# Hybrid decoder step on one core: the key scores of the dilated attention with the loop over the four column quarters innermost

## The chip, the cores and the metric

The kernel runs on one core of a Trainium2 chip. The metric is the device time of one launch in microseconds; the median of three runs before the change is 1605.24 us (1603.45 to 1611.88).

## What is computed

One inference step of a two-layer decoder trunk for a prompt (256 tokens) and a sample group (8 batches of 4 tokens), with the same weights: a gated-linear-attention layer, then a layer of dilated sliding-window attention over a shared key/value cache; each layer has a half-step SwiGLU feed-forward part before and after its mixer. The part that matters here is the attention of the samples. For each of the three window groups (distances 1, 4 and 16 between keys, 128 steps back) every sample token is scored against the cached keys:

```python
def dilated_group_sample(q, k_ctx, v_ctx, dil, steps, wb):
    T = q.shape[1]
    idx = wb + np.arange(T)[:, None] - dil * np.arange(steps + 1)[None, :]
...
    kg = k_ctx[:, idx]
    vg = v_ctx[:, idx]
    s = jnp.einsum('bthe,btjhe->bhtj', q, kg, preferred_element_type=jnp.float32) * DIL_SCALE
    p, lse = masked_softmax(s, jnp.asarray(valid)[None, None])
    o = jnp.einsum('bhtj,btjhe->bthe', p, vg.astype(jnp.float32))
    return o, lse.transpose(0, 2, 1)
```

Keys and values are read from cache_k and cache_v (8 batches, 2048 rows of 16 heads by 64), in float32.

## The kernel before

All weights and cache rows come through one stream of tiles, "raw", with 11 buffers (RAW_BUFS, class Stream). SyncE issues the transfers in the order of one job list; a transfer into a buffer waits until the work that last read it is done (for keys, TensorE's transposes at L1430; for values, TensorE's products at L1521). A job of cached rows is 1 MB or 0.75 MB and comes in two transfers of 512 KB (128 rows of 4 KB) or 384 KB (96 rows).

The samples' attention is a loop of 21 steps, x = 0 to 20 (L1542). Two batches are handled per iteration of four steps, so there are four iterations; the four steps of an iteration are (g, tp) = (1, 0), (1, 1), (2, 0), (2, 1), where g is the window group whose rows are loaded (the tiles of g = 1 serve the nearest group and part of the widest as well) and tp a pair of tokens. In a step:

- `keys` (L1420), called for each of the two batches (bp), takes the raw rows, transposes them on TensorE into PSUM (tile pa), ScalarE and VectorE copy them to kt, and GpSimd adds the new key's column (L1439).
- `key_scores` (L1442) multiplies the keys of the step before with the queries (tile qz, kept in the memory of xh and xl) into one PSUM bank, pb, and VectorE masks the result into Sc. It stands between the two calls of `keys`. There are eight calls with g = 1 and eight with g = 2.
- `pieces` (L1395) lets through one piece of the prompt's own attention (scores, softmax, spread, values), three times a step from x = 5 on.
- from x = 5 on, one of the four steps of `outputs` (L1511) multiplies weights with the values that the stream delivers five steps behind the keys.

The order of TensorE's products in this part is fixed: the helper `mm` (L1311, recorded at L1312) and `transpose` (L1314, recorded at L1315) pin each instruction behind the one written before it. So in the profile all products of this part stand at L1312 and all transposes at L1315, and the tiles tell them apart: pb<-kt are the key scores.

A product of the key scores has 32 columns of weights (queries of one batch and one half of the heads), and tile_position=(0, 32 * ...) puts it in one of the four 32-column quarters of the array; its output lies on the 32 partitions of that quarter. For each c4 (four pieces of 128 features) and each quarter there is one product when g = 2 (194 columns of keys), and there are three when g = 1: 258 columns, then 66, then 64 read with a step of four. Each float32 product is two passes on TensorE, each with a weight load of its own: a call with g = 1 is 48 products and 96 passes, a call with g = 2 is 16 products and 32 passes. A call is named a burst below.

```python
            for c4 in range(4):
                for hp in range(2):
                    for bp in range(2):
                        c, q = 4 * hp + c4, 32 * (2 * bp + hp)
```

Of the kernel before, what the change touches and what calls it, by code (L numbers as in the profile page):

```python
# [115 lines left out]
class Stream:  # L116
    """Raw tiles arrive in the order of the job list, by pieces; weights are split into two float32r parts."""
# [37 lines left out]
    def rows(self, i):  # L155
        """The raw pieces of a job and its k-th rows."""
        v = [self.raw.pop(x) for x in self.of[i]]
        return v, [t[:, k, :] for t in v for k in range(t.shape[1])]

    def part(self, low="dve"):  # L160
        """The next part of a weight split, if it is on its way."""
        x = self.parts[self.np]
        if x >= self.nd:
            return None
        self.np += 1
        i = self.pieces[x][0]
        self.split_part(self.split.setdefault(i, Weight()), self.jobs[i], self.raw.pop(x), f"{x}", low)
        self.freed.add(x)
        self.release()
        return True  # L170
# [10 lines left out]
    def aside(self, t, j):  # L181
        """A weight through a tile outside the stream."""
        v = t.rearrange("p (k c) -> p k c", c=j["nc"])
        self.load(v, j, 0, j["nk"])
        return v

    def prep(self, i):
        """All weights up to job i, as far as they are on their way."""
        self.pump()
        while self.np < len(self.parts) and self.pieces[self.parts[self.np]][0] <= i and self.part():  # L190
            pass

    def more(self, n, low="dve"):
        """The next n parts."""
        self.pump()
        while n and self.np < len(self.parts) and self.part(low):
            n -= 1

    def fill(self, limit=None):
        """The adaLN tiles that stand next in the list."""  # L200
        while self.nx < len(self.jobs) and self.jobs[self.nx]["kind"] == "ada":
            if limit is not None:
                if limit == 0:
                    return
                limit -= 1
            i = self.nx
            self.prep(i + 1)
            self.nx += 1
            self.handlers["ada"](self.jobs[i], self.rows(i)[1])
            self.free(i)  # L210
# [17 lines left out]
def weave(main, extra, lead=0, span=None):  # L228
    """extra spread evenly among main, after its first lead jobs."""
    if span is not None:  # L230
        return weave(main[:span], extra, lead) + main[span:]
    out = list(main[:lead])
    rest = main[lead:]
    n, m = len(rest), len(extra)
    k = 0
    for i, j in enumerate(rest):
        while k < m and k * n <= i * m:
            out.append(extra[k])
            k += 1
        out.append(j)  # L240
    out.extend(extra[k:])
    return out
# [64 lines left out]
def cache_job(I, name, g, b, tp, key):  # L307
    c = I[name][b].rearrange("s h e -> s (h e)")
    if g == 1:
        v = c[1536:2048, :].rearrange("(j t) f -> j t f", t=4)  # L310
    else:
        # the last 32 of the 128 rows stand in the first group's tiles too
        v = c.rearrange("(j t) f -> j t f", t=16)[0:J2]
    return dict(kind="r", key=key, src=v[:, 2 * tp:2 * tp + 2, :], nk=2, nc=D, rows=v.shape[0])


def body(tc, I, O, C, dbg=None):
# [17 lines left out]
    def bankB():  # L335
        return psB.tile([P, 512], F32, name=nm("pb"), tag="pb", bufs=3)
# [13 lines left out]
    # ---------------------------------------------------------------- constants and small inputs  # L350
# [23 lines left out]
    def pin(chain, ins):  # L374
        """Instructions of a chain keep their order on their engine."""
        last = chains.get(chain)
        if last is not None:
            tc.add_manual_dep(ins.ins, last.ins.name, mybir.DependencyInfo(mybir.DependencyClass.NoSync,
                              mybir.DependencyReason.DATA), reason="order")
        chains[chain] = ins  # L380
        return ins
# [54 lines left out]
    # ---------------------------------------------------------------- adaLN  # L436
# [37 lines left out]
    def ada_side(l, mod, tiles):  # L474
        """The first parts of an adaLN product, through tiles outside the stream."""
# [11 lines left out]
    def affine(gain, bias, l, msh, msc):  # L487
        """Scale and shift of modulate() after a LayerNorm's gain and bias."""
# [15 lines left out]
    def overlapped(m, last):  # L504
        """The steps of one chunk with the last step of the one before."""
        next(m)
        if last:
            next(last, None)
        next(m)
        return m  # L510

    def modulated(c, src, aff, hi, lo):
        """hi + lo = src * scale + shift, chunk c, in three steps."""
        s, b = aff
# [12 lines left out]
    # ---------------------------------------------------------------- products with a weight tile  # L527
# [13 lines left out]
    def project_chunkwise(group, xhi, xlo):  # L541
        """Several column tiles at once, chunk by chunk of x, as the chunks appear."""
# [4 lines left out]
    # ---------------------------------------------------------------- post-norm  # L547
    class Post:
        def __init__(self, g, late, eng):
            """The first chunks, late in number, come before the pivot."""  # L550
# [18 lines left out]
        def chunk(self, c, ps):  # L569
            zc = self.sublayer(c, ps)  # L570
            if c < 2:
                # a quarter of the features gives a pivot within two deviations of the mean
# [58 lines left out]
        def center(self, n):  # L631
            """The next weight's low part stands after n chunks."""
# [17 lines left out]
    class Final(Post):  # L650
        """The last LayerNorm, with the tokens on the partitions."""
# [37 lines left out]
        def finish(self):  # L689
            """Gain and bias: y * rstd + (bias - mean * rstd * gain), y with its gain already."""  # L690
# [23 lines left out]
    def post_norm(post, l, s, nxt):  # L714
        """nxt: list of (hi, lo); what is returned makes those after the first."""
# [23 lines left out]
    # ---------------------------------------------------------------- SwiGLU  # L739
    SIDE = {(0, 1): (0, 5), (0, 2): (1, 2), (1, 1): (1, 5)}  # L740

    def first_group(xh, xl):
        """The first products, as the shifts and scales of two chunks at a time arrive."""
# [127 lines left out]
    # ---------------------------------------------------------------- gated linear attention  # L871
    def gla(xh, xl):
# [9 lines left out]
        def flat(name, tag=None, bufs=1):  # L882
            """The prompt's rows of the four heads, then the samples' rows of the four heads."""
# [84 lines left out]
        def gram(x_k, x_q, idx, sidx):  # L968
            """The scores of one level, for the pairs that its mask names."""
# [52 lines left out]
        def decayed_keys():  # L1022
            """k times the decay from its row to the end of the rows."""
# [17 lines left out]
        def decayed_keys_t():  # L1041
# [8 lines left out]
            # the samples' rows four times over: high, high, low, low  # L1050
# [20 lines left out]
        def v_transposed(m, vt):  # L1071
# [12 lines left out]
            # the samples' rows four times over: high, low, high, low  # L1084
# [39 lines left out]
        # rows of the prompt  # L1124
# [32 lines left out]
        # rows of the samples, all heads and batches as one tile of rows  # L1157
# [37 lines left out]
        # normalization over a head's values, gate  # L1195
# [22 lines left out]
    # ---------------------------------------------------------------- shared keys and values  # L1218
    def rotate(ps, tab, outs):
        """Rotary encoding of two heads: the swapped halves by copies, their signs in the table."""  # L1220
# [62 lines left out]
    # ---------------------------------------------------------------- dilated attention  # L1283
    def dilated(KT, Vt, Vs, xh, xl):
# [25 lines left out]
        # the products of this part keep the order in which they stand here  # L1310
# [6 lines left out]
        # ---- the prompt, two heads at a time, in the two halves of the array  # L1317
        def scores(c):
            """In three steps."""
# [28 lines left out]
        def spread(c, i, e):  # L1348
            """The transposed weights of a head."""
# [52 lines left out]
        # ---- the samples, two batches at a time; rows are (batch, half of the heads, head, token)  # L1402
# [17 lines left out]
        def keys(pr, g, tp, bp):  # L1420
            """The transposed keys of two tokens, the new key behind them."""
# [20 lines left out]
        def key_scores(g, tp, kc, qz, Sc):  # L1442
            n = P + 1 if g == 1 else N2
            ps = bankB()
            for c4 in range(4):
                for hp in range(2):
                    for bp in range(2):
                        c, q = 4 * hp + c4, 32 * (2 * bp + hp)
                        k_ = kc[bp][hp][:, c4]
                        mm(ps[q:q + 32, 0:2 * n], lhsT=qz[:, g, c, bp, :], rhs=k_.rearrange("p u j -> p (u j)"),  # L1450
                           start=(c4 == 0), stop=(c4 == 3 and g == 2), tile_position=(0, q))
                        if g == 1:
                            mm(ps[q:q + 32, 258:324], lhsT=qz[:, 0, c, bp, :], rhs=k_[:, :, 96:129], start=False, stop=False,
                               tile_position=(0, q))
                            mm(ps[q:q + 32, 324:388], lhsT=qz[:, 2, c, bp, :], rhs=k_[:, :, 0:P:4], start=False,
# [17 lines left out]
        def softmax(pr, Sc):  # L1473
            """The weights: of the new rows, and for each token on the first group's tiles."""
# [5 lines left out]
            # on the first group's tiles: its own weights, the second group's last rows and the nearest rows  # L1480
# [5 lines left out]
            # the new rows: on the rows of all batches, zero where they belong to others  # L1486
# [24 lines left out]
        def outputs(pr, PT, W1, W2):  # L1511
            """In four steps, and the gathering of the heads."""
# [74 lines left out]
    # ---------------------------------------------------------------- the two layers  # L1587
# [76 lines left out]
```

## Time and profile before

| | |
|---|---|
| median of 3 runs | 1605.24 us |
| profiled execution: its own time, and its span | 1603.45 us, 1603.5 us |
| TensorE matmul busy | 1524.3 us, 95% |
| VectorE, ScalarE, GpSimd busy | 58%, 44%, 16% |
| granted clock, mean | 0.979 |
| transfers: bytes, mean rate | 342.72 MB, 214 GB/s |
| the cached rows (samples' attention), loop of 21 steps | about 1107 to 1323 us of the span |

The page gives busy time and share of each engine, the chain of work that ended last, and the costliest groups of instructions. PE is TensorE's matmul side and PEld its weight loads; because passes are pipelined and their ends modelled, a PE busy share near 1 does not say that the array streams all the time. A row of the window view has the stretch and its length, the busy time of PE, PEld, VectorE (DVE), ScalarE (ACT) and GpSimd (POOL) with their instructions, the granted clock, the busy share of the 16 DMA engines and the rate in GB/s at which they moved data. A row of the groups has line, engine, operation, tiles, shape and count, then busy time in us, the mean ns of one, and the idle time before it. The timeline merges consecutive instructions of one line and tile; "x96" is the number of passes.

### The profile page before, as it was taken

How to read it: one execution, taken by the hardware profiler on the slowest of the kernel's cores; microseconds unless marked ns; L12 is line 12 of the kernel's file. 1: busy time of each engine (PE TensorE's matmuls, PEld its weight loads, DVE VectorE, ACT ScalarE, POOL GpSimd, SP SyncE). 2: the span in 40 equal slices, each digit the busy share in tenths (PEclk: the TensorE clock that was granted, in tenths of full speed). 3: DMA queues.
4: the chain of work that ended last, by engine and by line, in shares of the span. 5: the costliest groups of instructions: out<-in, count | busy, mean ns of one | idle time of the engine just before them, and what ended most of it. 6: DMA issues, size and time to landing. Idle time of an engine off the chain costs nothing.

```text
span 1603.5 us, 31330 instructions
## 1 busy us (share of the span) xinstructions
PE 1524.3 (95%) x12564; PEld 1363.0 (85%) x12564; DVE 928.1 (58%) x1887; ACT 706.2 (44%) x1138; POOL 263.3 (16%) x408
## 2 busy tenths in 40 slices
PE   6999999999889999999999999899999988899996
PEld 4999997888869999988999999698766647899995
DVE  4544446596785444468544445765554577845556
ACT  2444333745635443336444434585333244444432
POOL 0000034002450000343000022424231112300001
PEclk8999999999989999999999999999999999999998
DMA  9966776545856677774556575775698996555430
GB/s 311 321 223 223 253 233 202 176 158 172 289 196 199 220 242 265 245 226 153 188 183 210 179 246 176 230 251 165 210 299 251 286 326 245 176 173 166 150 101 30
DMA packets 238820, 342.72 MB, mean 214 GB/s; under 512 B 12743, under 2 KB 202385, under 8 KB 238674
## 3 DMA queue, kind: packets, MB, share of 16 engines
q1 hardware_dynamic: 236210, 333.41, 64.4%
q0 software_dynamic: 2048, 7.14, 1.1%
q8 instruction: 98, 1.61, 0.4%
q14 instruction: 48, 0.39, 0.1%
q10 hardware_dynamic: 416, 0.17, 0.0%
HBM read 332.42 MB, written 8.26 MB: 212 GB/s over the span
## 4 chain that ended last, share of the span: by engine, by line
PE 82%; DVE 9%; DMA 4%; ACT 3%; issue 2%; POOL 1%; SPq 0%; DVEq 0%; ACTq 0%; POOLq 0%
PE pa L530 21%; PE pa L531 21%; PE pa L532 21%; PE pb L1312 5%; PE pd L449 3%; PE pa L1315 3%; PE pa L1312 2%; DMA raw<-in_cache_k_dram 1%; DMA raw<-in_w_ada_dram 1%; PE pa L973 1%; DVE z L639 1%; DVE lo L178 1%; DMA w<-in_w_ffn_up_dram 1%; DVE xm L516 1%; DVE xl L525 1%
## 5 line engine op out<-in xcount | busy, mean ns | idle before, releaser
L530 PE MATMUL pa<-xh,hi 128*128 128x288 f32 x1888 | 560.4, 301 | 12.9 <-ACT xh L523 9.5
L531 PE MATMUL pa<-xl,hi 128*128 128x288 f32 x1888 | 562.5, 298 | 3.1 <-DVE xl L525 2.6
L532 PE MATMUL pa<-xh,lo 128*128 128x288 f32 x1888 | 559.6, 297 | 3.9 <-DVE lo L178 3.9
L178 DVE TENSOR_TENSOR lo<-raw,hi 128x1024 fp32r<-128x1024 f32 (+1 forms) x345 | 414.4, 1209 | 226.8 <-ACT hi L176 220.0
L176 ACT ACTIVATE hi<-raw 128x1024 fp32r<-128x1024 f32 x350 | 358.6, 1035 | 254.5 <-PE pa L531 233.6
L530 PEld LDWEIGHTS pa<-xh,hi 128*128 128x128 f32 x1888 | 356.5, 190 | 26.6 <-ACT xh L523 10.4
L531 PEld LDWEIGHTS pa<-xl,hi 128*128 128x128 f32 x1888 | 359.1, 190 | 6.5 <-DVE xl L525 4.6
L532 PEld LDWEIGHTS pa<-xh,lo 128*128 128x128 f32 x1888 | 358.9, 190 | 5.4 <-DVE lo L178 4.9
L530 PE MATMUL pa<-hh,hi 128*128 128x288 f32 x704 | 209.6, 298 | 0.0
L532 PE MATMUL pa<-hh,lo 128*128 128x288 f32 x704 | 208.3, 296 | 0.0
L531 PE MATMUL pa<-hl,hi 128*128 128x288 f32 x704 | 208.0, 296 | 0.0
L810 DVE TENSOR_TENSOR sa<-pa,sa 128x288 f32<-128x288 f32 x88 | 39.7, 454 | 180.3 <-PE pa L532 174.5
L530 PEld LDWEIGHTS pa<-hh,hi 128*128 128x128 f32 x704 | 132.6, 188 | 4.3 <-issue 2.1
L532 PEld LDWEIGHTS pa<-hh,lo 128*128 128x128 f32 x704 | 132.4, 188 | 0.2
L531 PEld LDWEIGHTS pa<-hl,hi 128*128 128x128 f32 x704 | 132.4, 188 | 0.1
L811 ACT ACTIVATE hh<-sa 128x288 fp32r<-128x288 f32 x88 | 38.8, 445 | 133.9 <-DVE sa L810 131.0
L584 POOL TENSOR_TENSOR z<-z,lnpiv 128x288 f32<-128x288 f32 x6 | 4.7, 803 | 487.9 <-ACT lnpiv L579 487.9
L809 ACT ACTIVATE sa<-pa 128x288 f32<-128x288 f32 x88 | 35.0, 402 | 92.9 <-PE pa L532 92.8
L449 PE MATMUL pd<-raw,cT 128*32 128x256 f32 x1008 | 70.4, 384 | 4.4 <-ACT adas L455 4.4
L1435 ACT ACTIVATE kt<-pa 128x512 f32<-128x512 f32 (+1 forms) x64 | 34.4, 543 | 83.4 <-PE pa L1315 70.1
L1315 PEld LDWEIGHTS pa<-ident,raw 128*128 128x128 f32 (+1 forms) x512 | 50.1, 141 | 20.5 <-issue 8.0
L1315 PE MATMUL pa<-ident,raw 128*128 128x128 f32 (+1 forms) x512 | 59.8, 265 | 4.2 <-DVE kt L1433 1.6
(354 smaller groups left out, 1839.3 us busy)
## 6 DMA issues: line engine op xcount, KB each, us to landing
raw<-in_w_ffn_up_dram SPq DMA_DIRECT2D x172, 512.0 KB, 5.0
raw<-in_w_ada_dram SPq DMA_DIRECT2D x110, 512.0 KB, 4.9
raw<-in_w_ffn_down_dram SPq DMA_DIRECT2D x80, 512.0 KB, 4.8
raw<-in_cache_k_dram SPq DMA_DIRECT2D x32, 512.0 KB, 7.5
raw<-in_cache_v_dram SPq DMA_DIRECT2D x32, 512.0 KB, 7.5
raw<-in_w_in_a_dram SPq DMA_DIRECT2D x24, 512.0 KB, 5.3
raw<-in_w_q_b_dram SPq DMA_DIRECT2D x24, 512.0 KB, 4.5
raw<-in_cache_k_dram SPq DMA_DIRECT2D x32, 384.0 KB, 8.4
```

The costliest lines, as they stand in the source:

```text
L176: self.pin("act", self.nc.scalar.activation(hv, src, AF.Copy))
L178: self.pin(low, eng.tensor_tensor(out=lo, in0=src, in1=hv.bitcast(F32), op=ALU.subtract))
L449: T.matmul(ps[32 * q:32 * q + 32, :], lhsT=cT[:, k, :], rhs=raw[kk][:, 256 * q:256 * q + 256], start=(k == 0), stop=(k == DC - 1), tile_po ...
L530: ins = [T.matmul(ps, lhsT=whi, rhs=xhi, start=first, stop=False), T.matmul(ps, lhsT=whi, rhs=xlo, start=False, stop=False), T.matmul(ps, ...
L531: T.matmul(ps, lhsT=whi, rhs=xlo, start=False, stop=False),
L532: T.matmul(ps, lhsT=wlo, rhs=xhi, start=False, stop=last)]
L809: A.activation(sa, pa[:, 0:NT], AF.Silu)
L810: V.tensor_tensor(out=sa, in0=pu[:, 0:NT], in1=sa, op=ALU.mult)
L811: A.activation(hh[:, m, :], sa, AF.Copy)
L1312: pin("pe", T.matmul(*a, **k))
L1315: pin("pe", T.transpose(*a))
L1435: A.activation(dst, pt, AF.Copy)
```

## The change

The loop over the four quarters becomes the innermost one. Before, the three products of a quarter follow each other and then comes the next quarter; after, the first product of all four quarters, then the second of all four, then the third. The products, their operands, their start and stop flags and the bank stay as they are. With g = 2 there is one product per quarter and the order is the old one. The diff also strips comments and docstrings elsewhere in the file, which moves no instruction.

```diff
         def key_scores(g, tp, kc, qz, Sc):
             n = P + 1 if g == 1 else N2
             ps = bankB()
+            quarters = [(hp, bp) for hp in range(2) for bp in range(2)]
+
             for c4 in range(4):
-                for hp in range(2):
-                    for bp in range(2):
+                for kind in range(3 if g == 1 else 1):
+                    for hp, bp in quarters:
                         c, q = 4 * hp + c4, 32 * (2 * bp + hp)
                         k_ = kc[bp][hp][:, c4]
-                        mm(ps[q:q + 32, 0:2 * n], lhsT=qz[:, g, c, bp, :], rhs=k_.rearrange("p u j -> p (u j)"),
-                           start=(c4 == 0), stop=(c4 == 3 and g == 2), tile_position=(0, q))
-                        if g == 1:
+                        if kind == 0:
+                            mm(ps[q:q + 32, 0:2 * n], lhsT=qz[:, g, c, bp, :], rhs=k_.rearrange("p u j -> p (u j)"),
+                               start=(c4 == 0), stop=(c4 == 3 and g == 2), tile_position=(0, q))
+                        elif kind == 1:
                             mm(ps[q:q + 32, 258:324], lhsT=qz[:, 0, c, bp, :], rhs=k_[:, :, 96:129], start=False, stop=False,
                                tile_position=(0, q))
+                        else:
                             mm(ps[q:q + 32, 324:388], lhsT=qz[:, 2, c, bp, :], rhs=k_[:, :, 0:P:4], start=False,
                                stop=(c4 == 3), tile_position=(0, q))
```

TensorE, first burst with g = 1 (step x = 1), its first c4; kt_12144 and kt_12145 hold the two halves of the heads of batch 0, kt_12176 and kt_12177 those of batch 1, so the four names are the four quarters; 32x258, 32x66 and 32x64 are the three products:

```order
 L1312 MATMUL pb_12240<-kt_12144,xh_12117 32x258
+L1312 MATMUL pb_12240<-kt_12176,xh_12117 32x258
+L1312 MATMUL pb_12240<-kt_12145,xh_12117 32x258
+L1312 MATMUL pb_12240<-kt_12177,xh_12117 32x258
 L1312 MATMUL pb_12240<-kt_12144,xh_12117 32x66
+L1312 MATMUL pb_12240<-kt_12176,xh_12117 32x66
+L1312 MATMUL pb_12240<-kt_12145,xh_12117 32x66
+L1312 MATMUL pb_12240<-kt_12177,xh_12117 32x66
 L1312 MATMUL pb_12240<-kt_12144,xh_12117 32x64
-L1312 MATMUL pb_12240<-kt_12176,xh_12117 32x258
-L1312 MATMUL pb_12240<-kt_12176,xh_12117 32x66
 L1312 MATMUL pb_12240<-kt_12176,xh_12117 32x64
```

The products of the other three quarters with 258 columns move up ahead of the first quarter's shorter ones; four quarters now stand side by side in each kind.

TensorE, the end of the same burst in the changed kernel and the transposes behind it (raw_11893 and raw_12039 are key rows of the step's second batch):

```order
L1312 MATMUL pb_12240<-kt_12145,xh_12117 32x66
L1312 MATMUL pb_12240<-kt_12177,xh_12117 32x66
L1312 MATMUL pb_12240<-kt_12144,xh_12117 32x64
L1312 MATMUL pb_12240<-kt_12176,xh_12117 32x64
L1312 MATMUL pb_12240<-kt_12145,xh_12117 32x64
L1312 MATMUL pb_12240<-kt_12177,xh_12117 32x64
L1315 MATMUL pa_12314<-ident,raw_11893 128x128
L1315 MATMUL pa_12314<-ident,raw_12039 128x128
```

What stands behind the burst is unchanged. The rows of SyncE, ScalarE, VectorE and GpSimd are in the old order too; the only wait that moves is that of the products with kt_12176 and kt_12177 for GpSimd's new-key columns, which now stand second and fourth in the burst, not fourth and tenth.

## Rows read from the trace of the kernel before

**Rows 1.** The page's head and its first part, busy time by engine.
```profile
span 1603.5 us, 31330 instructions
PE 1524.3 (95%) x12564; PEld 1363.0 (85%) x12564; DVE 928.1 (58%) x1887; ACT 706.2 (44%) x1138; POOL 263.3 (16%) x408
```

**Rows 2.** Windows over the samples' attention: busy time by engine, clock, DMA share, GB/s.
```profile
1110.00:1180.00 70.00, 68.55 (x778) 50.95 (x780) 35.07 (x113) 21.69 (x45) 21.04 (x86) 1.00 0.71 213
1180.00:1230.00 50.00, 48.73 (x510) 31.67 (x506) 25.53 (x102) 14.59 (x32) 10.34 (x36) 1.00 0.91 281
1230.00:1310.00 80.00, 76.16 (x798) 46.77 (x792) 49.69 (x191) 30.34 (x72) 12.98 (x35) 1.00 1.01 301
1310.00:1330.00 20.00, 15.72 (x94) 7.35 (x95) 14.45 (x46) 11.40 (x24) 2.48 (x4) 0.85 1.06 366
```

**Rows 3.** Timeline of TensorE, 1115 to 1135 and 1126 to 1148 us: bursts and transposes.
```profile
1115.15 7.94 PE L1312 MATMUL pb<-kt,xh 128*32 128x258 f32 x96
1123.03 3.48 PE L1315 MATMUL pa<-ident,raw 128*128 128x128 f32 x32
1126.43 7.94 PE L1312 MATMUL pb<-kt,xh 128*32 128x258 f32 x96
1134.31 3.14 PE L1315 MATMUL pa<-ident,raw 96*128 96x96 f32 x32
1137.38 1.52 PE L1312 MATMUL pb<-kt,xh 128*32 128x194 f32 x32
```

**Rows 4.** Groups by shape, 1110 to 1330 us: passes and weight loads of the key scores.
```profile
L1312 PE MATMUL pb<-kt,xh 128*32 128x258 f32 x128 | 30.4, 393 | 0.0
L1312 PE MATMUL pb<-kt,xl 128*32 128x64 f32 x128 | 25.1, 286 | 0.0
L1312 PE MATMUL pb<-kt,xl 128*32 128x66 f32 x128 | 17.8, 220 | 0.0
L1312 PE MATMUL pb<-kt,xl 128*32 128x194 f32 x128 | 6.6, 330 | 1.1 <-ACT kt L1435 1.1
L1312 PEld LDWEIGHTS pb<-kt,xl 128*32 128x32 f32 x512 | 26.1, 109 | 13.2 <-issue 1.8 <-POOL pe L1342 1.8
```

**Rows 5.** What SyncE's transfers wait for, 1110 to 1310 us: us, times, longest.
```profile
SPq L144 <- PE pa L1315: 113.2, 40, 11.4
SPq L144 <- PE pa L1312: 21.4, 14, 5.9
```

**Rows 6.** What TensorE waits for, 1110 to 1310 us: us, times, longest.
```profile
PE pa L1315 <- DVE kt L1433: 1.6, 3, 0.8
PE pb L1312 <- ACT kt L1435: 1.1, 1, 1.1
...
PE pa L1315 <- DMA raw<-in_cache_k_dram: 0.3, 1, 0.3
```

**Rows 7.** The chain that ended last, in order of time, around 1230 us.
```profile
1230.71 7.72 DMA raw<-in_cache_k_dram
1238.49 12.20 DMA raw<-in_cache_k_dram
```

**Rows 8.** Instructions of GpSimd's line 1439, 1110 to 1310 us: who waited for it.
```profile
  POOL kt L1439: 10.2, 1
  ACT kt L1435: 2.6, 2
  PEld pb L1312: 0.2, 1
```

**Rows 9.** Windows in which TensorE is often idle: same columns as Rows 2.
```profile
1320.00:1330.00 10.00, 7.49 (x34) 4.78 (x35) 7.90 (x17) 6.96 (x14) 0.00 (x0) 0.70 1.06 403
1350.00:1360.00 10.00, 5.89 (x42) 4.98 (x44) 9.93 (x18) 4.87 (x7) 3.51 (x3) 1.00 0.43 130
1360.00:1370.00 10.00, 6.38 (x74) 3.33 (x66) 7.77 (x12) 3.69 (x8) 7.11 (x7) 0.92 0.71 225
```

## The prediction, made before the changed kernel was run

> **What bounds the kernel now.** I read the page's busy times first [rows 1]: TensorE is busy for 95% of the span, far ahead of every other engine, so work taken from it can count. That is an average; what a saving is worth must be read where it falls. The change touches only the key scores, so the second view is the window view of the samples' attention [rows 2], where the reader is to see two different limits in one stage. From 1110 to 1180 us TensorE is busy for 68.55 of 70 us while the DMA engines are busy for 0.71 of the time at 213 GB/s: TensorE sets the pace. From 1230 to 1310 us the DMA share is 1.01 at 301 GB/s: the transfers of the cached rows are at their limit, and TensorE, with 76.16 of 80 us, is only just as long. Between them, 1180 to 1230, the share is 0.91. The third view is who waits for whom. SyncE's transfers wait 113.2 us for TensorE's transposes to give a raw buffer back and 21.4 us for the value products [rows 5], while TensorE waits next to nothing, 0.3 us of it for cached keys [rows 6]. So TensorE drives the transfers; but the chain that ended last already runs through two transfers of cached keys, 7.72 and 12.20 us, at 1230 us [rows 7]. Both limits are close to each other there.
>
> **The bursts now.** A burst with g = 1 takes 7.94 us for 96 passes and one with g = 2 takes 1.52 us for 32 [rows 3]. Per pass that is 83 ns against 47 ns. The longer products of g = 1 (258 columns, not 194) cannot be the reason, since two thirds of its passes have only 64 or 66 columns. The g = 2 burst is the one whose order already has the quarters innermost. A wave there, one pass in each of the four quarters, takes (1.52 - 0.33) / 7 = 0.170 us, with 0.33 us for the last pass [rows 3, 4]: 0.88 ns per column, for four quarters together. In the g = 1 burst, two passes of 258 columns at that rate are 0.45 us, and 7.94 us over 16 (four c4, four quarters) is 0.50 us: the long products of the quarters run one after another, and only the short ones hide beside the next quarter's.
>
> **The change, step by step.** It removes and adds no instruction. It turns the 96 passes of each of the eight bursts with g = 1 into 24 waves: 8 of 258 columns, 8 of 66 and 8 of 64.
>
> - Waves of 258 columns: 8 x 258 x 0.88 ns = 1.81 us.
> - Short waves: at the same rate 8 x 66 and 8 x 64 columns are 0.91 us. No wave this short stands alone before, so I bound it from the other side by the weight load of 109 ns [rows 4], as if no wave could be shorter than one load: 16 x 0.109 = 1.74 us. The 64-column pass, which reads with a step of four, also lasts longer than the 66-column one, 286 against 220 ns [rows 4], so the truth is probably not at the lower end.
> - The last pass: 0.29 us.
>
> A burst becomes 3.0 to 3.84 us; I take 3.4, in the middle. That is 4.5 us less (4.1 to 4.9), and 36 us over eight bursts, as TensorE's own work. The far end, in which the short waves do not overlap at all, is a rival below.
>
> Edits that cost nothing: two of a burst's first four products now stand earlier than before in front of a wait for GpSimd's new-key column. The scores are those of the step before, so the columns are there; TensorE's weight loads waited 0.2 us for that line in 200 us [rows 8]. If that cover went, it would be about 1 us a burst at most, since the fourth quarter was reached within 1.4 us before too. VectorE takes the scores out of the bank after the last product, as before. VectorE and ScalarE have over a third of the stage free [rows 2], and SyncE's order is the old one.
>
> **What of the 36 us reaches the end.** Four bursts lie in the first part (1115, 1126, 1148 and 1166 us; the first two in [rows 3]) and four in the second. Take the bytes: 213 x 70 + 281 x 50 + 301 x 80 gives 53.0 MB of cached rows moved from 1110 to 1310 us [rows 2].
>
> First part: TensorE gets 4 x 4.5 = 18 us shorter. The transfers of those 70 us, 14.9 MB, need 49.5 us at 301 GB/s, so there are 20.5 us of room. The 18 us fit: buffers come free earlier, SyncE's waits of [rows 5] shorten, and the transfers follow.
>
> Second part: another 18 us fall off TensorE, but the 14.05 MB of the stretch from 1180 to 1230 need 46.7 us at 301 GB/s, 3.3 us of room, and 1230 to 1310 has none. So nearly all of this half is turned into TensorE waiting for raw rows. I count the 3.3 us as nothing, because the mean rate of 1180 to 1310, hiccups included, is 38.1 MB in 130 us, 293 GB/s; held from 1110 on, it takes 181 us for the 53.0 MB, 19 us less than now. That second way to the sum ends at the same place as the first.
>
> From 1310 to 1330 us nothing changes: the transfers stay full (1.06) and the last heads of the prompt go through VectorE and ScalarE.
>
> The sum: 18 us, half of what TensorE saves. The profiled execution has a span of 1603.5 us [rows 1] and would have 1585.5; it lies 1.7 us below the median of the runs shown, so I forecast 1605.2 - 18 = **1587.2 us**.
>
> **A rule that speaks against it.** The trace shows for g = 2 that the loads of the four quarters overlap with each other and with passes under way: 32 loads of 109 ns would be 3.5 us in line, and the whole burst takes 1.52 [rows 3, 4]. The Trainium skill (TensorE: Matmul & The Clock Gate, Part 3, on what overlaps) says that a weight load overlaps with matmuls in flight only where the row group differs, and here all quarters use all rows. By that rule the bursts could not get below 96 loads in line, before or after; the trace does not agree with it.
>
> **Rivals.**
>
> 1. *The transfers do not follow.* In the first part they come in groups of one batch's rows with a pause behind each, and if each pause keeps part of its length because SyncE issues again only when TensorE has transposed, the share may rise from 0.71 to 0.85 and not to 1: the 70 us become 58.5 at most, and with TensorE's other limits I price this at 3 to 9 us, about 1599 us. For it: TensorE's own work per step in the first steps is then about as long as its transfers. Against it: with 11 buffers the share is 1.01 later on. Chance 0.14.
> 2. *More than the DMA sum allows.* If the rate can go well above 301 GB/s (366 from 1310 on [rows 2]), up to 36 us are free: 1569 to 1580 us. Against it: the 301 GB/s are already at a share of 1.01 with this mix of rows. Chance 0.06.
> 3. *The order does not matter.* If the quarters were held up by something that both orders share, such as the one bank that all write, the bursts stay at 7.94 us: 1605 us. Against it: the g = 2 burst writes one bank as well. Chance 0.05.
> 4. *Slower: weight loads in line.* Before, the short passes hide beside the next quarter's long one. After, 64 short passes stand together, with some 57 ns of columns to hide a load of 109 ns. If those loads go one behind another, they take 64 x 0.109 = 7.0 us, with the long waves 8.8 us, with the last pass 9.1: 1.2 us more than now, 9 us over eight bursts, 1614 us. It decides once a short pass costs over (7.94 - 0.29 - 1.81) / 64 = 91 ns. Against it stands the g = 2 burst with 47 ns per pass. Chance 0.04.
> 5. *Slower: the clock.* TensorE would have 193 - 36 = 157 us of work in some 181 us of stage. If its clock fell to half for long in the gaps, the slack of 24 us and the gain of 18 would be gone after 84 us at half clock. Against it: with 5.89 and 6.38 us busy of 10 the granted clock was 1.00 and 0.92; the 0.70 of 1320 to 1330 is the worst near here [rows 9]. Chance 0.01.
>
> **How the numbers follow.** The forecast case, 12 to 25 us less, has 0.70. About 0.5% (8 us) is what a measurement of this kernel can tell from no change; half of rival 1 lies within it. Faster: 0.70 + 0.06 + 0.07 = 0.83. Same: 0.07 + 0.05 = 0.12. Slower: 0.05. The range takes the forecast case from a loss-free 27 us (the whole DMA pause of 20.5 and 3.3 us with some 3 us of the last stretch) down to 7 us, in rival 1: 1578 to 1598 us. It leaves out most of rivals 2 to 5.
>
> **What would show it.** In the changed profile the bursts with g = 1 should stand in the timeline with about 3.4 us for 96 passes. The DMA share from 1110 us on should be near 1 until the last values are in, at about 300 GB/s; SyncE's wait for transposes should be well under 113 us; TensorE should wait some 15 to 20 us for cached keys and values, where it was 0.3. The first out-projection behind the loop should start about 18 us earlier and everything behind it be shifted by that. I am wrong if bursts stay above 6 us (rivals 3 and 4), if they are short and the DMA share stays under 0.9 in the first part (rival 1), or if the rate rises far above 301 GB/s (rival 2).

## The result and the profile after

The changed kernel takes 1588.8 us, median of 4 runs (1581.38 to 1590.35); the kernel before, on the same chip, takes 1608.56 us, median of 4 (1603.45 to 1612.12). The ratio is 0.9878, with a 95% interval from 0.985 to 0.9907: 15 to 24 us less, where 18 (and 1587.2 us) had been forecast. The profiled execution has a span of 1588.1 us, 15.4 less than that of [rows 1].

The page of the changed kernel, head and busy times:

```profile
span 1588.1 us, 31330 instructions
PE 1499.7 (94%) x12564; PEld 1344.7 (85%) x12564; DVE 929.9 (59%) x1887; ACT 705.4 (44%) x1138; POOL 260.8 (16%) x408
```

TensorE is busy for 24.6 us less. The timeline of TensorE stands against [rows 3]; its last line is burst 5, the first of the second four:

```profile
1114.93 3.36 PE L1312 MATMUL pb<-kt,xh 128*32 128x258 f32 x76
1119.29 0.97 PE L1312 MATMUL pb<-kt,xh 128*32 128x258 f32 x20 [0.99 <-POOL xh L1416]
1120.19 3.48 PE L1315 MATMUL pa<-ident,raw 128*128 128x128 f32 x32
1123.60 3.36 PE L1312 MATMUL pb<-kt,xh 128*32 128x258 f32 x96
...
1129.95 1.52 PE L1312 MATMUL pb<-kt,xh 128*32 128x194 f32 x32
...
1186.91 3.36 PE L1312 MATMUL pb<-kt,xh 128*32 128x258 f32 x96
```

A burst of 96 passes is now 3.36 us long, from 7.94; that of g = 2 is the old one. Eight bursts are 36.6 us shorter (8 x 4.58). The busy time fell by less, since other products of the stage cover more time than before: those of the 96-row values (pa<-raw,xl) 22.4 us, from 17.0. The first burst is cut in two by a wait of 0.99 us for a copy on GpSimd, of which more below. The groups by shape, 1100 to 1330 us, each of them half of the eight bursts, against [rows 4]:

```profile
L1312 PE MATMUL pb<-kt,xl 128*32 128x258 f32 x128 | 10.3, 390 | 0.0
L1312 PE MATMUL pb<-kt,xl 128*32 128x64 f32 x128 | 6.8, 287 | 0.0
L1312 PE MATMUL pb<-kt,xl 128*32 128x66 f32 x128 | 4.9, 220 | 0.0
```

A single pass is as long as before (390, 287 and 220 ns against 393, 286 and 220). What fell is the busy time that a group covers: 30.4 to 10.3 us for the long passes, 17.8 and 25.1 to 4.9 and 6.8 for the short. The passes run beside one another.

The windows of the samples' attention, same columns as [rows 2]:

```profile
1110.00:1180.00 70.00, 65.68 (x920) 48.92 (x922) 44.02 (x153) 26.54 (x56) 24.52 (x99) 1.00 0.93 275
1180.00:1230.00 50.00, 43.01 (x494) 26.73 (x494) 23.84 (x82) 16.32 (x37) 10.12 (x34) 0.90 1.03 297
1230.00:1310.00 80.00, 71.44 (x745) 38.90 (x737) 52.63 (x203) 30.48 (x70) 12.16 (x29) 0.96 1.01 296
1310.00:1330.00 20.00, 18.96 (x127) 18.18 (x127) 13.97 (x30) 8.21 (x15) 1.42 (x2) 0.91 0.92 351
```

The DMA share is 0.93 from 1110 us on, where it was 0.71, and over 1 from 1180 to 1310, at 296 to 297 GB/s. TensorE is idle for 7 of the 50 us from 1180 on. What SyncE's transfers wait for, 1110 to 1310 us, against [rows 5]:

```profile
SPq L144 <- PE pa L1315: 68.0, 37, 10.3
SPq L144 <- DMA raw<-in_cache_v_dram: 41.0, 42, 1.9
...
SPq L144 <- PE pa L1312: 17.7, 18, 3.9
```

And what TensorE's products wait for in the same stretch, against [rows 6]:

```profile
PE pa L1315 <- DMA raw<-in_cache_k_dram: 7.5, 7, 2.1
PE pa L1312 <- DMA raw<-in_cache_v_dram: 5.4, 6, 2.3
```

The transfers wait 68.0 us for TensorE's transposes, not 113.2; TensorE waits 12.9 us for cached rows, not 0.3. So part of the waiting has moved from the transfers to TensorE. The chain that ended last agrees. Around 1230 us it held two transfers of cached keys in [rows 7]; here are pieces of it between 1160 and 1302 us, in order of time:

```profile
1161.89 10.37 DMA raw<-in_cache_k_dram
1172.32 12.67 DMA raw<-in_cache_k_dram
1185.05 12.84 DMA raw<-in_cache_k_dram
1197.95 13.38 DMA raw<-in_cache_k_dram
1211.41 12.57 DMA raw<-in_cache_k_dram
...
1248.88 14.19 DMA raw<-in_cache_k_dram
...
1288.31 12.56 DMA raw<-in_cache_v_dram
```

From 1162 to 1224 us it is transfer behind transfer.

### The profile page after: what moved, and what is told of

Read it like the earlier page. It is cut to its first block, busy times and chain, and to the rows that moved or that the text cites. A ratio compares the mean times of both kernels' runs of the same rounds, so it can differ in the third digit from the quotient of the medians.

```text
span 1588.1 us, 31330 instructions
## 1 busy us (share of the span) xinstructions
PE 1499.7 (94%) x12564; PEld 1344.7 (85%) x12564; DVE 929.9 (59%) x1887; ACT 705.4 (44%) x1138; POOL 260.8 (16%) x408
## 4 chain that ended last, share of the span: by engine, by line
PE 79%; DVE 8%; DMA 7%; ACT 3%; issue 2%; POOL 1%; SPq 0%; DVEq 0%; ACTq 0%
PE pa L530 22%; PE pa L531 21%; PE pa L532 21%; DMA raw<-in_cache_k_dram 5%; PE pd L449 3%; PE pa L1315 2%; PE pb L1312 2%; PE pa L1312 1%; DVE xm L516 1%; PE pa L973 1%; DVE z L639 1%; DMA raw<-in_cache_v_dram 1%; DVE xl L525 1%; DVE lo L178 1%; DMA raw<-in_w_ada_dram 1%
## 5 line engine op out<-in xcount | busy, mean ns | idle before, releaser
L1315 PEld LDWEIGHTS pa<-ident,raw 128*128 128x128 f32 (+1 forms) x512 | 53.1, 146 | 27.6 <-issue 10.3
L1315 PE MATMUL pa<-ident,raw 128*128 128x128 f32 (+1 forms) x512 | 63.2, 274 | 11.1 <-DMA raw<-in_cache_k_dram 7.5
L1435 ACT ACTIVATE kt<-pa 128x512 f32<-128x512 f32 (+1 forms) x64 | 34.1, 541 | 74.3 <-PE pa L1315 65.9
```

The source lines that it names most:

```text
L1315: pin("pe", T.transpose(*a))
L1435: A.activation(dst, pt, AF.Copy)
```

## Experiments

All were timed against the kernel before on the same chip. Beside the time, one number is read from the one profile of each kernel: the **stage time**, from the start of the first burst to the end of the span. It leaves out what happens ahead of the first burst, whose start lies anywhere between 1114.2 and 1120.3 us in these profiles, and differs even between kernels that are the same up to there. For the kernel before it is 1603.5 - 1115.15 = 488.35 us [rows 1, 3], for the changed one 1588.1 - 1114.93 = 473.17: 15.2 less. It stands for one execution: the changed kernel and the one with the new order in the first half alone have the same instructions up to burst 5, which starts 72.0 us behind burst 1 in the one profile and 74.4 in the other. Where transfers set the pace, differences of 2 or 3 us between stage times therefore mean little.

| kernel | median us (95% interval of the ratio to before) | stage time against before |
|---|---|---|
| changed | 1588.8 (0.985 to 0.9907) | -15.2 |
| new order in the first two iterations | 1593.56 (0.99 to 0.9942) | -7.8 |
| new order in the last two iterations | 1602.68 (0.9966 to 1.0) | -5.3 |
| changed, rows for g = 2 16 KB apart | 1586.31 (0.9856 to 0.9906) | -22.0 |
| before, rows for g = 2 16 KB apart | 1608.12 (1.0005 to 1.0033) | -0.1 |
| changed, 128 rows for g = 2 | 1570.8 (0.9757 to 0.9802) | -34.1 |
| before, 128 rows for g = 2 | 1606.75 (0.9991 to 1.0018) | 0.0 |
| 128 rows, first two iterations | 1592.06 (0.989 to 0.9934) | -15.8 |
| 128 rows, last two iterations | 1586.78 (0.986 to 0.9898) | -17.7 |
| only the long products together | 1594.83 (0.9883 to 0.9942) | -12.1 |
| quarters outermost for g = 2 | 1597.36 (0.9916 to 0.9964) | -9.7 |

**The halves apart.** The new order in the first four bursts alone, then in the last four alone (`it >= 2`).

```diff
-        def key_scores(g, tp, kc, qz, Sc):
+        def key_scores(g, tp, kc, qz, Sc, new):
...
+            order = [(k, a) for k in kinds for a in quarters] if new else [(k, a) for a in quarters for k in kinds]
...
-                late = (g, tp, kc, qz[it], Sc[it])
+                late = (g, tp, kc, qz[it], Sc[it], it < 2)
```

> The new order only in the first two iterations (the four bursts of the first part), the old one in the last two. Theory D (the transfers of cached rows take back what the last four bursts save): as fast as the changed kernel, 17 to 20 us below the kernel before; last four bursts 7.9 us long, and TensorE waits for cached rows less than in the changed kernel. Rival P (every burst is worth the same, the shortfall is spread over all eight): about 10 us below before.

> The new order only in the last two iterations, the old one in the first two. Theory D: 1 to 5 us below before, since from 1180 us on the transfers had only some 3 to 5 us of room. Rival P: about 10 us below before.

The first half alone: 1593.56 us against 1604.64, ratio 0.9921 (0.99 to 0.9942), 9 to 16 us less. The last half alone: 1602.68, ratio 0.9983 (0.9966 to 1.0), 0 to 5.5 us less. So the last half is worth less than rival P's 10 us, as theory D has it. The first half is worth more than the last, but less than theory D's 17 to 20 us; by itself it fits rival P as well. TensorE waits 4.2 us for cached rows with the first half alone, 12.9 in the changed kernel. The windows of the first kernel, and behind them the last two of the second:

```profile
1110.00:1180.00 70.00, 65.24 (x919) 49.20 (x917) 44.41 (x144) 27.90 (x59) 24.71 (x93) 1.00 0.89 256
1180.00:1230.00 50.00, 46.88 (x472) 28.81 (x468) 25.88 (x99) 16.18 (x37) 13.15 (x42) 0.97 0.93 267
1230.00:1310.00 80.00, 76.03 (x770) 44.27 (x762) 47.09 (x191) 26.07 (x61) 9.42 (x25) 1.00 0.97 291
```

```profile
1180.00:1230.00 50.00, 48.09 (x585) 30.04 (x583) 30.18 (x117) 19.48 (x45) 12.05 (x41) 1.00 0.99 300
1230.00:1310.00 80.00, 72.42 (x771) 42.87 (x770) 47.69 (x178) 26.85 (x63) 11.75 (x31) 0.91 1.03 296
```

The first window opens 8.7 us ahead of burst 1 here; over the 65 us from burst 1 on, the share is 0.98 (0.96 in the changed kernel, 0.73 before). With the old bursts behind the new ones, the share falls back to 0.93 and 0.97: the long bursts make the transfers pause again, and some of the lead is lost. The timeline of TensorE in the first kernel shows it, at bursts 1 (its first piece), 5 and 8, and behind it bursts 5 and 8 of the kernel before:

```profile
1118.74 3.39 PE L1312 MATMUL pb<-kt,xh 128*32 128x258 f32 x76
...
1193.17 7.94 PE L1312 MATMUL pb<-kt,xh 128*32 128x258 f32 x96
...
1262.70 7.94 PE L1312 MATMUL pb<-kt,xl 128*32 128x258 f32 x96
```

```profile
1200.37 7.94 PE L1312 MATMUL pb<-kt,xh 128*32 128x258 f32 x96
...
1267.90 7.94 PE L1312 MATMUL pb<-kt,xl 128*32 128x258 f32 x96
```

Burst 5 starts 74.4 us after burst 1, where the kernel before takes 85.2 (1200.37 - 1115.15): a lead of 10.8 us. At burst 8 it is 144.0 against 152.75 (1267.90 - 1115.15), 8.8 us; at the end of the span, 7.8. The lead melts. In the other kernel the share is 0.99 and 1.03 as soon as the last four bursts are 4.5 us shorter, and little comes out.

**Are the transfers slow because of the rows' distance?** The theory that the transfers take the other half back needs a kernel in which they are faster. Rows for g = 2 lie 64 KB apart; here they lie 16 KB apart, in the changed kernel and in that before. The samples' g = 2 scores and values are then those of other rows.

```diff
-        v = c.rearrange("(j t) f -> j t f", t=16)[0:J2]
+        v = c[0:4 * J2, :].rearrange("(j t) f -> j t f", t=4)
```

> The changed kernel, with the 96 rows of the tiles of g = 2 read 16 KB apart in memory and not 64 KB apart; other rows than the reference's are read, so what the samples' scores of g = 2 and their values are computed from changes. Theory D: 384 KB come in about 1.05 us and not 1.75, 64 of them free some 40 us of transfers, TensorE sets the pace again and the rest of the 36 us appears: 30 to 40 us below before. Rival V (VectorE, ScalarE or GpSimd between the products hold the second half): stays at 18 to 22 us below before.

> The kernel before with the same rows 16 KB apart. Theory D: TensorE was busy for 193 of the 200 us, so faster transfers alone give little, 2 to 7 us below before; the two orders then differ by 28 to 36 us. Rival V: the two orders differ by 20 us or less.

1586.31 us, ratio 0.9881 (0.9856 to 0.9906), for the first, the same as the changed kernel; 1608.12, 1.0019 (1.0005 to 1.0033), for the second. Neither time is the one that theory D gave. The windows of the first tell why:

```profile
1180.00:1230.00 50.00, 45.19 (x543) 28.56 (x534) 27.25 (x102) 18.20 (x41) 13.40 (x43) 0.97 1.03 307
1230.00:1310.00 80.00, 70.65 (x734) 37.12 (x730) 54.03 (x205) 30.99 (x72) 12.26 (x29) 0.98 1.04 310
```

The rate is 307 and 310 GB/s at a full share, not 297 and 296, and the stage time is 6.8 us below the changed kernel's: the transfers became a little faster at most. So theory D's condition, transfers of 1.05 us, was not met, and the time that rival V gave (18 to 22 us) came out with transfers almost as slow as before: the pair decides nothing between them. It does say that the distance of the rows is not the main thing that makes them slow.

**Faster transfers: 128 rows.** What is left is that a transfer for g = 2 fills 96 partitions and one for g = 1 all 128. Here g = 2 loads 128 rows, of which the first 96 are used as before; a third more bytes for it.

```diff
-        v = c.rearrange("(j t) f -> j t f", t=16)[0:J2]
+        v = c.rearrange("(j t) f -> j t f", t=16)[0:P]
...
-                        transpose(pt[:, f, u, :], raw[u][:, P * c:P * c + P], ident[0:n, 0:n])
+                        transpose(pt[:, f, u, :], raw[u][0:n, P * c:P * c + P], ident[0:n, 0:n])
...
-                               rhs=rr[bp][2][u][:, 512 * hp:512 * hp + 512],
+                               rhs=rr[bp][2][u][0:P if g == 1 else J2, 512 * hp:512 * hp + 512],
```

> The changed kernel, with 128 rows loaded for the tiles of g = 2 and only the first 96 of them used: a third more bytes in these transfers, spread over all 128 partitions. The run with rows 16 KB apart left the packets of the 96-row transfers at 250 ns, against 159 ns of the 128-row ones, so their distance in memory is not why they are slow. Theory D (transfers set the pace of the second half) with the cause in the 96 partitions: these transfers fall from about 1.7 to 1.35 us, 64 of them free over 20 us, and 8 to 14 us appear, 27 to 34 us below before. Rival V (VectorE, ScalarE or GpSimd hold the second half): 17 to 21 us below before. Rival B (bytes count, not partitions): a third more bytes at the old rate, 2.3 us each, 0 to 10 us below before or slower.

> The kernel before with the same 128 rows loaded. Theory D: TensorE sets the pace for most of the stage, so 2 to 8 us below before; with e5 the two orders then differ by 24 to 30 us, against 19 us with 96 rows. Rival V: the orders still differ by 19 us. Rival B: 15 us or more above before.

With the new order: **1570.8 us**, median of 4 runs, against 1607.4, ratio 0.9779 (0.9757 to 0.9802). That is 32 to 39 us less than before, the whole of the 36 us of TensorE work, and somewhat more than theory D gave (27 to 34). Rivals V and B are out. With the old order: 1606.75, ratio 1.0004 (0.9991 to 1.0018), nothing, where theory D gave 2 to 8 us. The faster transfers alone are worth nothing; they decide what the saving is worth. The windows, first with the new order, then with the old:

```profile
1110.00:1180.00 70.00, 67.32 (x938) 49.33 (x942) 45.01 (x158) 27.89 (x61) 25.55 (x102) 1.00 0.92 335
1180.00:1230.00 50.00, 47.71 (x654) 31.30 (x650) 32.20 (x119) 19.15 (x42) 9.64 (x34) 1.00 1.00 388
1230.00:1310.00 80.00, 72.09 (x692) 46.58 (x685) 55.81 (x190) 34.27 (x75) 11.98 (x26) 0.96 0.97 374
```

```profile
1180.00:1230.00 50.00, 48.19 (x518) 32.00 (x518) 25.11 (x95) 15.06 (x33) 10.34 (x36) 1.00 0.85 328
1230.00:1310.00 80.00, 76.49 (x802) 46.44 (x802) 50.20 (x191) 30.25 (x71) 12.84 (x35) 1.00 0.93 347
```

388 GB/s at a share of 1.00, with the old order 0.85 and 0.93. What TensorE waits for in the fast kernel, 1110 to 1290 us, its longest rows:

```profile
PE pa L1315 <- DVE pe L1344: 3.0, 5, 1.3
PE pa L1315 <- DVE kt L1433: 2.4, 4, 1.5
PE pb L1312 <- ACT kt L1435: 1.1, 1, 1.1
```

The cached rows are gone from the list. The rate in forty slices from 1230 to 1290 us shows which transfers were slow; first the changed kernel, then the one with 128 rows:

```profile
GB/s 361 374 385 276 339 360 303 295 262 235 249 270 276 366 401 314 262 249 246 249 251 251 243 251 257 262 249 249 265 276 300 325 423 418 421 393 268 262 243 281
```

```profile
GB/s 407 429 415 421 415 412 423 418 418 410 415 418 410 410 426 418 412 415 418 418 423 412 423 421 421 347 145 369 229 259 412 393 380 382 384 386 384 386 393 412
```

With transfers of both kinds the rate goes up and down between about 250 and about 420 GB/s at a share that stays full; with 128 rows alone it holds near 415 until the queue runs dry at 1268. The single 4 KB pieces say the same: from 1180 to 1290 us, 96% of them take 159 ns with 128 rows, but 31% in the changed kernel, where the median is 228 ns.

**The halves apart, with 128 rows.** The two edits above together: the new order in two of the four iterations, on the fast transfers.

> 128 rows loaded for the tiles of g = 2, the new order only in the first two iterations. Theory D (with the transfers out of the way every burst is worth its 4.5 us): 15 to 20 us below before, the other half of the 35 us comes with the last two iterations. Rival: as with 96 rows, about 12 us.

> 128 rows loaded for the tiles of g = 2, the new order only in the last two iterations. Theory D: 14 to 19 us below before, where it was 2.7 us with 96 rows; with e9 the two halves add up to the 35 us of all eight bursts. Rival R (the last four bursts lie in a part that something other than the transfers holds): 2 to 6 us below before.

First half: 1592.06 us against 1604.61, ratio 0.9912 (0.989 to 0.9934), 11 to 18 us less, and 15.8 us of stage time. Last half: 1586.78, ratio 0.9879 (0.986 to 0.9898), 16 to 22 us less, and 17.7 us. Each half takes 18.3 us off TensorE. The last half is now worth that, and rival R is out. The time of the first half lies between its two forecasts (15 to 20, and about 12) and decides nothing; the places of its bursts 1 (first piece), 5 and 8 do:

```profile
1119.80 3.40 PE L1312 MATMUL pb<-kt,xh 128*32 128x258 f32 x76
...
1189.64 7.94 PE L1312 MATMUL pb<-kt,xh 128*32 128x258 f32 x96
...
1256.76 7.94 PE L1312 MATMUL pb<-kt,xl 128*32 128x258 f32 x96
```

The lead on the kernel before is 15.4 us at burst 5 (85.2 - 69.8) and stays: 15.8 at burst 8 and at the end, where with 96 rows it fell from 10.8 to 7.8. Up to burst 5 TensorE waits 4.0 us where it waited 1.6 before, none of it for cached rows: 1.0 for GpSimd's copy of queries and 2.5 (from 1.1) for the copies of keys on VectorE and ScalarE. That is most of what is missing from 18.3. The stage times of the two halves, 33.5 us together, add up to the 34.1 of both. The windows of the last half's kernel:

```profile
1110.00:1180.00 70.00, 68.55 (x777) 51.04 (x780) 34.97 (x113) 21.57 (x45) 20.93 (x86) 1.00 0.68 242
1180.00:1230.00 50.00, 46.90 (x598) 29.76 (x587) 31.23 (x119) 19.45 (x44) 13.70 (x46) 1.00 1.00 384
1230.00:1310.00 80.00, 73.22 (x792) 41.83 (x791) 57.11 (x211) 35.15 (x79) 12.15 (x29) 0.94 1.02 398
```

The same four bursts gave 2.7 us of time (1 - 0.9983 of 1605) at 296 to 300 GB/s, and give 19.4 (1 - 0.9879 of 1605) at 384 to 398. That is the clearest pair of the study: same edit, same saving on TensorE, another transfer rate.

**Which passes have to stand together?** First only the long products of the four quarters side by side, the short ones quarter by quarter as before; then the changed kernel with the quarters outermost in the bursts of g = 2, which had them innermost all along.

```diff
+            order = [(0, a) for a in quarters] + ([(k, a) for a in quarters for k in (1, 2)] if g == 1 else [])
...
-                for kind in range(3 if g == 1 else 1):
-                    for hp, bp in quarters:
+                for kind, (hp, bp) in order:
```

```diff
-            for c4 in range(4):
-                for kind in range(3 if g == 1 else 1):
-                    for hp, bp in quarters:
+            order = [(c4, kind, a) for c4 in range(4) for kind in range(3) for a in quarters]
+            if g == 2:
+                order = [(c4, 0, a) for a in quarters for c4 in range(4)]
+            for c4, kind, (hp, bp) in order:
...
```

> The changed kernel with only the 258-column products of the four quarters side by side; the 66 and 64 columns follow quarter by quarter. If quarters overlap only where their products stand next to each other, a burst takes 1.8 + 16 x 0.25 us and more, 5.5 to 7 us; if TensorE looks some instructions ahead, 4 to 5 us. By theory D the time follows the bursts of the first part: 5.5 to 7 us gives 5 to 10 us below before, 4 to 5 us gives 12 to 18.

> The changed kernel with the opposite order in the bursts of g = 2: the quarters outermost, the four c4 of a quarter one after another. If standing side by side is what makes the quarters overlap, these bursts go from 1.52 us to 4 x 8 x 0.16 + 0.33 = 5.5 us, 32 us more of TensorE's work over eight bursts, and the kernel gives back 13 to 20 us of the gain: 0 to 7 us below before. If not, it stays 17 to 21 us below.

The timelines of TensorE, of the first and of the second kernel:

```profile
1128.17 3.43 PE L1312 MATMUL pb<-kt,xh 128*32 128x258 f32 x96
```

```profile
1132.10 3.58 PE L1312 MATMUL pb<-kt,xh 128*32 128x194 f32 x32
```

With the long products together a burst is 3.43 us, 0.07 more than with all of them and less than either forecast: the short ones need no rearranging. The time, 1594.83 (ratio 0.9912, 0.9883 to 0.9942), has an interval that overlaps that of the changed kernel; the two can't be told apart by it. With the quarters outermost, the burst of g = 2 goes from 1.52 to 3.58 us, not to the 5.5 forecast: the quarters still overlap in part. The order is thus the cause in both kinds of burst, in either direction. The kernel takes 1597.36 us (0.994, 0.9916 to 0.9964): eight bursts with 2.06 us more are 16.5 us of TensorE work, of which 5.5 show in the stage time (15.2 against 9.7) and some 10 in the ratios (0.994 against 0.9878 of 1605 us): again only a part reaches the end.

## Why the prediction was right, point by point

- **The burst.** 3.4 us forecast, 3.36 measured. Eight long waves of 1.81 us together and the last pass of 0.29 leave 1.26 us for sixteen short waves, 79 ns each, where the bound by the load was 109 and that by the columns 57. The starts of single passes in the trace show that this is a mean of two kinds: in the burst at 1123.60 the two 66-column waves start at 1124.055 and 1124.115 us, the two 64-column ones at 1124.173 and 1124.275, and the next long one at 1124.392. So the 66 columns take some 60 ns, the columns' rate, and the 64 columns, read with a step of four, 102 and 117, about as long as a load; whether the step or the load makes them so long is not separated. Rivals 3 and 4 are out. Of the rule that it was weighed against (the Trainium skill, TensorE: Matmul & The Clock Gate, Part 3) the changed trace says the same as [rows 3, 4] did: a load there takes 113 ns, and 96 in line would be 10.8 us, where the burst takes 3.36.
- **The first part.** The share rose to 0.93 (0.96 over the 65 us from burst 1 on), TensorE's saving turned into earlier transfers, and rival 1 (the pauses stay) is out: burst 5 starts 72.0 us after burst 1 (1186.91 - 1114.93), 13.2 us sooner than before. It is not the 18 us of the sum. Some 3 us of the difference are not due to the transfers: with 128 rows, too, the lead at burst 5 is only 15.4. The rest fits TensorE's waits for cached rows ahead of burst 5, 1.8 us.
- **The second part.** "Another 18 us fall off TensorE", of which nothing counts: that nearly held, and the runs show the reason given for it to be the true one. On slow transfers these four bursts are worth 0 to 5.5 us, on fast ones 16 to 22. Of the signs named, TensorE's wait for cached rows is 12.9 us, below the 15 to 20 forecast, and the out-projection behind the loop starts 14.8 us sooner (1311.61, from 1326.42), not 18; what follows keeps that shift.
- **What was off.** The sum put all 18 us down to the first part and none to the second. Shown is about 12.7 and 2.7 (ratios 0.9921 and 0.9983 of 1605 us) for either alone. In the changed kernel's profile 13.2 us are there at burst 5, and 2.0 come behind it. So two errors of the sum are of opposite sign: the first part brings less than its 18 us, and the second, whose 3.3 us of room were counted as nothing, brings some 2 (0 to 5.5 in the runs with the last half alone). That the sum came out so near owes something to luck; that one half counts and the other hardly does is no luck.
- **Edits at nothing.** The wait of two early products for GpSimd's new-key column, priced at nothing, does not show. Another wait does that was not named: in the first burst 76 passes run, then TensorE waits 0.99 us for GpSimd's copy of queries (line 1416), then 20 passes follow. Before, the burst itself was long enough to cover that copy. It happens once and costs at most 1 us.
- **The clock.** Rival 5's mechanism is there. A window of the changed kernel, same columns as [rows 2]:

```profile
1220.00:1230.00 10.00, 7.34 (x54) 5.52 (x58) 1.38 (x2) 2.18 (x4) 0.00 (x0) 0.66 1.04 264
```

  The granted clock is 0.66, a mean between the two levels of 1.2 and 2.4 GHz, in ten microseconds in which TensorE stood idle for cached keys for 2.3 us in two waits. Its price is not separated. It is small at most: the DMA share of 1.04 says that the transfers set the pace there, and the mean granted clock of the whole execution is 0.979, as before. With the new order in the last two iterations alone, the runs have a mean clock of 0.976 where the kernel before has 0.979; 0.003 of 1605 us is 5 us, an estimate of the most that the clock could take from that half. Going to 128 rows brings that half 17 us. In the kernel with 128 rows and all bursts in the new order, the clock is 1.00 from 1180 to 1230.
- **Rival 2**, more than the transfers allow, is out for this kernel (296 to 297 GB/s at a full share). Its time, 1569 to 1580 us, is what the kernel with 128 rows reaches, 1570.8 us, by lifting that rate.

## What to carry to other kernels

Where products use separate column quarters of the array, issue the long ones of the four quarters side by side; the short ones fill in by themselves. Price such a saving against the other limit of the same stage, by bytes over the rate at a full DMA share: what lies beyond it turns into waiting, and lifting the second limit can then pay in full, as here (32 to 39 us), although it paid nothing alone. A transfer that fills fewer than all partitions can cost more time than one with a third more bytes that fills them.

## What the runs showed of the hardware that was not expected

- Transfers of 96 rows onto 96 partitions run at about 250 GB/s with the DMA share full, those of 128 rows at about 415, with rows of the same 4 KB pieces; rows 16 KB apart instead of 64 changed that little. By these rates 512 KB takes 1.3 us and 384 KB 1.6. The Trainium skill (SBUF — State Buffer, Door 1: The DMA port swizzle) says that the partition number decides the port, and that partitions 0 to 63 reach only half of the 16 ports. By that rule, an estimate: of 96 rows 64 fall on one half of the ports and 32 on the other, so they go at three quarters of the full rate, 311 of 415 GB/s. No run here shows the ports. The trace agrees in direction and shows a larger loss, to 0.6; what the rest is stays open.
- TensorE starts products of another quarter ahead of ones that stand earlier in the program. The bursts of 3.43 us with the short products still quarter by quarter show it, and so do those of 3.58 us for g = 2 with the quarters outermost: 32 passes of 194 columns in line, at the 0.170 us of [rows 3, 4], would be 5.4 us. The starts of single passes in the trace show how far ahead. In the first burst of the kernel before, the second quarter's first long pass starts at 1115.618 us, beside the first quarter's first short one (1115.612); three passes of the first quarter start only behind it (1115.672, 1115.729, 1115.827). With the quarters outermost for g = 2, a second row of passes starts at 1132.790, beside the fifth of the first quarter's eight passes (1132.785): again three are left. So in the old order the long passes of the next quarter come up only when those of the quarter before have all started, and the four quarters' long passes run in line, one quarter every 0.465 us. Why it is three, and whether it is so elsewhere, was not tested.
